# Splits, ropes, partial sums and an activation table issued in another order in a retention/GLA decoder layer

## The chip, the core and the metric

The kernel runs on one core of one Trainium2 chip. The metric is device time in microseconds (us) of one execution; several executions are timed and the median is given. A core has engines that run side by side, each with its own queue in program order: TensorE (PE, with its weight loads PEld), VectorE (DVE), ScalarE (ACT), GpSimd (POOL), and SyncE (SP), which here only issues DMAs. POOL issues DMAs too, those that add into their destination among them.

## The reference

One layer over 528 positions (16 meta tokens and 512 of the sequence), width 1024, float32:

```python
u = rms_norm(h, norm_gain)
proj = u @ w_in
(rq, rk, rv, rg, gq, gk, gv, gg, glr, m_ret, m_gla) = jnp.split(proj, points, axis=-1)
rq = rope(rq, pos); rk = rope(rk, pos) * RET_QK_DIM ** -0.5
o_ret = head_group_norm(retention_chunked(rq, rk, rv), ret_norm_gain) * silu(rg)      # 4 heads
log_a = log_sigmoid(glr @ w_gate_up + b_gate) / GLA_GATE_TAU
o_gla = head_rms_norm(gla_chunked(gq * GLA_K_DIM ** -0.5, gk, gv, log_a), gla_norm_gain) * silu(gg)
merged = sigmoid(m_ret) * (o_ret @ w_branch_ret) + sigmoid(m_gla) * (o_gla @ w_branch_gla)
h = h + merged @ w_out
return rms_norm(h, final_norm_gain)[:, N_META:]
```

## The kernel before

Every product of float32 operands is made from three matmuls: `split(hi, lo, src)` (L154) rounds a tile on ACT (`scalar.copy`, the CAST rows of L155) and takes the rest on DVE (`tensor_sub`, the TENSOR_TENSOR rows of L155); PE then multiplies hi by hi, hi by lo and lo by hi. Weights come from DRAM by SP in tiles of 512 KB (`wraw`, six buffers) and are split into `whi` and `wlo` (`wsplit`, three buffers each).

Most projections go through `quad` (L253): it computes a block of two column tiles over two token halves with seven products, each on sums of weight blocks, as in Strassen's scheme, where eight would be plain. `product(i, ...)` splits its weight block and issues 24 matmuls of 256 columns. The products come in the order 1, 2, 6, 7, 5, 4, 3, with a `yield` behind each. The sums of weight blocks (`w11 += x3`, L320; `w21 += w11`, L325) are DVE additions, and partial results are copied from a bank of PSUM by ACT (`copy`, L300) before the bank is used further: the bank of products 1, 6, 5 and 3 is `b`, that of 7 and 4 is `c`. `proj_a` (L350) is the plain projection used for the first pair of GLA heads, q (gq0) and then k (gk0): 96 matmuls each.

The text of the kernel is made of generators. `weave(dense, chain)` (L205) advances `chain` by one step after each step of `dense`, so that chains of small operations (gates, rope, scores, attention) lie between dense matmuls. `tick` (L233), called once at each dense step, counts down the entries of the list `pend` and calls those at zero, from the head of the list on, stopping at the first that is not due. A planner orders each engine's queue: it takes the operations by their place in this text and by when its own model of costs has their inputs ready. `after(ins, prev)` pins one instruction behind another on the same engine; `act` and `vec` chain instructions so with the last of their engine in `ends`, and `qsplit` is a split whose two halves are chained so.

The places that matter here, in order of time:

- The forget gates of GLA (`forget_gates`, L641): z = glr @ w_gate_up in five matmuls, then for each of the five blocks Abs, Exp and Identity on ACT and two operations on DVE, then a scaling of gv (L674) and five Ln on ACT with a DVE subtraction each (L678). This chain is woven into `gla_qk(0)`; gk0's two weight halves are split inside `proj_a`, behind the chain's z blocks. The next dense stage is the first output gate of GLA, `gla_g(0)` (names gg).
- For each retention head h: `ret_qk(h)` (names rqk) woven with the attention of the head before; `ret_rope(h)` (rpk, rpq, on DVE), `ret_g(h)` (output gate, names rg), `ret_v(h)` (names rv) and `ret_scores(h)`. The attention of a head has six steps: four blocks of values (av) and two of `turn` (L426), which transposes on PE (ot) and splits on ACT and DVE (oh L439, ol L440). For h = 0 and h = 3 the gate and values are the dense part, and rope runs through `every(gen, 3, 2)`, which puts a pause behind each two steps.
- `gates_ret` (L1124, names mr): the last gates. `part` (L1131) reads partial sums kr from DRAM, multiplies by the gate on DVE (L1132) and adds the product back by a POOL DMA. The sums of the first two pairs are due 4 and 5 ticks after the start, the others 2 ticks after their gate. `gate` (L894) evacuates a product, scales it and applies Sigmoid (L898).

Of the kernel before, what the change touches and what calls it, by code (L numbers as in the profile page):

```python
# [11 lines left out]

# [8 lines left out]
F32 = mybir.dt.float32  # L21
# [6 lines left out]
P = 128  # L28
# [79 lines left out]
def hybrid_kernel(ctx: ExitStack, tc: tile.TileContext, I, out: bass.AP):  # L108
# [105 lines left out]
    def every(gen, n, m=1):  # L214

        for i, _ in enumerate(gen):
            yield
            if i % m == m - 1:
                for _ in range(n - m):
                    yield  # L220
# [32 lines left out]
    def quad(cols, rows, name, evac, meta=None, adds=True):  # L253
# [26 lines left out]
        def product(i, form, w, ps, fresh):  # L280
            hi, lo = wsplit([P, 4, 256], f"{name}_{i}")
            split(hi, lo, w)
            for t in range(2):
                col = slice(t * P, (t + 1) * P)
                for kk in range(4):
                    u = [f[form][:, kk, col] if rows else f[form][:, kk, :256] for f in (fh, fl)]
                    v = [f[:, kk, :] if rows else f[:, kk, col] for f in (hi, lo)]
                    first = fresh and kk == t == 0
                    for j, (x1, x2) in enumerate(((0, 0), (0, 1), (1, 0))):
                        l, r = (u[x1], v[x2]) if rows else (v[x1], u[x2])  # L290
                        m = nc.tensor.matmul(ps[:, t, :], l, r, start=first and j == 0, stop=kk == 3 and j == 2,  # L291
                                             skip_group_check=not fresh or t == 1)
                        if t == kk == j == 0:
                            pin(m)
            order[:] = [m]
# [17 lines left out]
        run_late()  # L313
        yield
# [4 lines left out]
        product(2, A12, w21, a, True)  # L319
# [30 lines left out]
    def proj_a(col, meta, name, evac):  # L350
# [8 lines left out]
        for kh in range(2):  # L359
            if (name, kh) not in loaded:  # L360
                load_a(col, kh, name)
            if (name, kh) not in parts:
                parts[name, kh] = wsplit([P, 4, 256], f"{name}_{kh}")
                (qsplit if name == "gk0" else split)(*parts[name, kh], loaded.pop((name, kh)))
# [276 lines left out]
    def forget_gates():  # L641
# [11 lines left out]
        yield  # L653
        for b in range(5):
# [6 lines left out]
            nc.scalar.activation(e, ps, AF.Abs)  # L661
            nc.scalar.activation(e, e, AF.Exp, scale=-1.0)

            nc.scalar.activation(w1, e, AF.Identity, bias=one)
            nc.vector.scalar_tensor_tensor(w1, w1, 1.0, e, op0=ALU.subtract, op1=ALU.subtract)
# [3 lines left out]

        for _ in range(4):  # L670
            yield
        last = ends["act"]
# [285 lines left out]
    def rope(t, c, name):  # L958
# [5 lines left out]
        nc.vector.tensor_mul(m[0], t[:, 0], c[0])  # L964
        nc.vector.tensor_mul(m[1], t[:, 1], c[1])
# [22 lines left out]
    def ret_rope(h):  # L988
        q, k = R["raw", h]
        yield from rope(k, (cs[:, 0], cs[:, 1]), f"rpk{h}")  # L990
# [16 lines left out]
    def ret_g(h):  # L1007
        sg = rp.tile([P, NTB, 512], F32, tag="sg", name=f"sg{h}")
        R["sg", h] = sg
        yield from quad((C_RG + h * 512, C_RG + h * 512 + 256), True, f"rg{h}", rows_into(sg, AF.Silu))  # L1010
# [113 lines left out]
    def gates_ret():  # L1124
# [6 lines left out]
        def part(k, c, s):  # L1131
            nc.vector.tensor_mul(k, k, sigr[c][:, :, s])  # L1132
            collect(kept[:, 2 * c:2 * c + 2, s], k, False)

        for c in range(2):
            k = rp.tile([P, 2, T], F32, tag=("sh", "sl")[c], name=f"kr{c}")
            nc.gpsimd.dma_start(k, kept2[:, 2 * c:2 * c + 2, :])
            pend.append((4 + c, lambda c=c, k=k: part(k, c, slice(0, T))))

# [25 lines left out]
    for h in range(4):  # L1165
        if h == 0:
            drain(ret_qk(h))
        else:
            weave(ret_qk(h), ret_attention(h - 1))
# [4 lines left out]
        else:  # L1174
            weave(run(ret_g(h), ret_v(h)), run(every(ret_rope(h), 3, 2), ret_scores(h)))
# [97 lines left out]
```

## Time and profile before

| what | value |
|---|---|
| median of 3 runs | 792.84 us (792.55 to 793.69) |
| profiled execution | 790.81 us, its span 789.0 us |
| PE busy in the span | 770.7 us (98%) |
| PEld | 700.0 us (89%) |
| DVE | 571.7 us (72%) |
| ACT | 450.1 us (57%) |
| POOL | 143.5 us (18%) |
| granted PE clock, mean | 0.994 |

A busy PE is counted while a matmul is in its pipeline, so 98% says how little of the span PE stood with nothing to do, not that it ran at its peak. A row of a timeline reads: start, duration, engine, line, operation, output<-inputs, shape, how many in a row; in brackets the idle time of the engine before it and what ended it.

### The profile page before, as it was taken

The page shows a single profiled execution, that of the slowest core. Times are in us where ns is not written, and L with a number is a line of the kernel's source. Part 1 is how long each engine was busy: PE and PEld are TensorE (multiplying, and loading weights), DVE is VectorE, ACT ScalarE, POOL GpSimd, SP SyncE. Part 2 cuts the span into 40 slices and gives each one's busy share as a digit, 9 for nine tenths or more (in the row PEclk, how much of TensorE's full clock was granted, in tenths as well). Part 3 has the DMA queues.
Part 4 walks back from the last instruction along what each step waited for, and adds up shares of the span by engine and source line. Part 5 has one row for each costly group of instructions (what it writes and reads, how often), then busy time and mean ns, then how long its engine had stood idle before and what let it go on. Part 6 is the DMA issues. An engine that isn't in the chain of part 4 may idle for free.

```text
span 789.0 us, 13628 instructions
## 1 busy us (share of the span) xinstructions
PE 770.7 (98%) x5404; PEld 700.0 (89%) x5404; DVE 571.7 (72%) x824; ACT 450.1 (57%) x744; POOL 143.5 (18%) x200
## 2 busy tenths in 40 slices
PE   9989999999999999999999999999999899989996
PEld 6779989999888899999989999889999898888885
DVE  5858688677654579788977688977686988577832
ACT  8887775577555456645646545646445655363422
POOL 2310120101312313100320100340011101333031
PEclk9989999999999999999999999999999999999999
DMA  9882503653138983833585463695465326799202
GB/s 283 263 206 46 141 5 105 142 142 91 67 124 198 252 189 108 184 110 107 168 246 145 111 160 108 160 237 138 123 150 129 101 88 205 118 310 313 94 2 107
DMA packets 94600, 117.91 MB, mean 149 GB/s; under 512 B 5956, under 2 KB 80580, under 8 KB 94280
## 3 DMA queue, kind: packets, MB, share of 16 engines
q1 hardware_dynamic: 74456, 85.32, 35.4%
q0 software_dynamic: 19936, 31.46, 20.7%
q8 instruction: 42, 0.69, 0.4%
q10 hardware_dynamic: 144, 0.26, 0.1%
q14 instruction: 22, 0.18, 0.1%
HBM read 99.20 MB, written 17.83 MB: 148 GB/s over the span
## 4 chain that ended last, share of the span: by engine, by line
PE 85%; DVE 6%; ACT 3%; DMA 2%; issue 2%; POOL 1%; POOLq 0%; SPq 0%; DVEq 0%; ACTq 0%
PE rv_b L291 6%; PE rg_b L291 5%; PE rqk_b L291 4%; PE br_p L193 4%; PE br_p L194 4%; PE br_p L190 4%; PE mg_b L291 3%; PE gv_p L557 3%; PE rg_c L291 3%; PE rv_c L291 2%; PE gg_b L291 2%; PE rqk_c L291 2%; PE mr_b L291 2%; PE bg_p L190 2%; PE bg_p L194 2%; PE bg_p L193 2%
## 5 line engine op out<-in xcount | busy, mean ns | idle before, releaser
L194 PE MATMUL br_p<-oh,br_l 128*128 128x512 f32 x128 | 50.5, 395 | 0.0
L193 PE MATMUL br_p<-ol,br_h 128*128 128x512 f32 x128 | 50.5, 395 | 0.0
L190 PE MATMUL br_p<-oh,br_h 128*128 128x512 f32 x128 | 50.5, 395 | 0.0
L155 ACT CAST rv_h<-rv_w 128x1024 fp32r<-128x1024 f32 x24 | 25.2, 1052 | 28.0 <-DVE rv_w L320 10.1
L891 POOL DMA_DIRECT2D kept<-mt x24 | 20.4, 849 | 110.5 <-ACT mt L1153 110.5
L1093 ACT ACTIVATE on<-av,nm,g_r 128x512 f32<-128x512 f32 x16 | 12.5, 779 | 48.6 <-DVE nm L1091 48.6
L155 DVE TENSOR_TENSOR rv_l<-rv_w,rv_h 128x1024 fp32r<-128x1024 f32 x24 | 29.3, 1222 | 8.8 <-ACT rv_h L155 8.8
L155 DVE TENSOR_TENSOR rg_l<-rg_w,rg_h 128x1024 fp32r<-128x1024 f32 x20 | 24.4, 1220 | 7.9 <-ACT rg_h L155 7.9
L194 PEld LDWEIGHTS br_p<-oh,br_l 128*128 128x128 f32 x128 | 24.0, 187 | 5.8
L193 PEld LDWEIGHTS br_p<-ol,br_h 128*128 128x128 f32 x128 | 24.0, 188 | 5.2
L190 PEld LDWEIGHTS br_p<-oh,br_h 128*128 128x128 f32 x128 | 24.0, 188 | 5.1
L271 POOL DMA_DIRECT2D rqk_x<-in_w_in_dram x8 | 10.4, 1306 | 98.6 <-DVE vl L155 83.1
L155 DVE TENSOR_TENSOR rqk_l<-rqk_w,rqk_h 128x1024 fp32r<-128x1024 f32 x20 | 24.4, 1219 | 5.1 <-ACT rqk_h L155 5.1
L291 PE MATMUL rg_b<-rg_l,fh 128*128 128x256 f32 x96 | 27.0, 282 | 0.3 <-DVE rg_l L155 0.3
L155 ACT CAST rg_h<-rg_w 128x1024 fp32r<-128x1024 f32 x20 | 21.0, 1052 | 11.0 <-PE br_p L193 5.0
L291 PE MATMUL rqk_b<-fh,rqk_l 128*128 128x256 f32 x96 | 27.1, 283 | 0.1
L291 PE MATMUL rqk_b<-fh,rqk_h 128*128 128x256 f32 x96 | 27.2, 283 | 0.0
L291 PE MATMUL rqk_b<-fl,rqk_h 128*128 128x256 f32 x96 | 27.0, 282 | 0.0
L291 PE MATMUL rv_b<-rv_h,fl 128*128 128x256 f32 x96 | 27.0, 282 | 0.0
L291 PE MATMUL rv_b<-rv_l,fh 128*128 128x256 f32 x96 | 27.0, 281 | 0.0
L291 PE MATMUL rg_b<-rg_h,fh 128*128 128x256 f32 x96 | 27.0, 281 | 0.0
L291 PE MATMUL rv_b<-rv_h,fh 128*128 128x256 f32 x96 | 27.0, 281 | 0.0
(646 smaller groups left out, 3171.6 us busy)
## 6 DMA issues: line engine op xcount, KB each, us to landing
rv_w<-in_w_in_dram SPq DMA_DIRECT2D x16, 512.0 KB, 4.1
br_w<-in_w_branch_ret_dram SPq DMA_DIRECT2D x16, 512.0 KB, 3.7
rqk_w<-in_w_in_dram SPq DMA_DIRECT2D x12, 512.0 KB, 5.0
rg_w<-in_w_in_dram SPq DMA_DIRECT2D x12, 512.0 KB, 4.0
kept<-mt POOLq DMA_DIRECT2D x24, 256.0 KB, 5.1
bg_w<-in_w_branch_gla_dram SPq DMA_DIRECT2D x8, 512.0 KB, 3.9
mr_w<-in_w_in_dram SPq DMA_DIRECT2D x8, 512.0 KB, 3.7
kept<-gb POOLq DMA_DIRECT2D x16, 256.0 KB, 4.1
```

What stands on the lines that cost most here:

```text
L155: return nc.scalar.copy(hi, src), nc.vector.tensor_sub(lo, src, hi.bitcast(F32))
L190: m = nc.tensor.matmul(o, lh, rh, start=first, stop=False)
L193: nc.tensor.matmul(o, lh, rl, start=False, stop=False)
L194: m = nc.tensor.matmul(o, ll, rh, start=False, stop=last)
L271: nc.gpsimd.dma_start(t, block(0, 1), accum_op=ALU.add)
L291: m = nc.tensor.matmul(ps[:, t, :], l, r, start=first and j == 0, stop=kk == 3 and j == 2, skip_group_check=not fresh or t == 1)
L557: m = nc.tensor.matmul(pss[t], (al if j == 1 else ah)[t // 2, kh][:, k, c], (lo if j == 2 else hi)[:, kk, :], start=q == kk == j == 0, sto ...
L891: nc.gpsimd.dma_start(dst, t, **({} if first else {"accum_op": ALU.add}))
L1093: nc.scalar.activation(on, ps, AF.Identity, scale=r, bias=nm)
```

## The change

Four edits. The split of both k weight halves (gk0) moves from `proj_a` into `forget_gates`, ahead of the z matmuls, one half to a step; the Abs and the first DVE operation of each gate block are pinned behind the last of these splits; four empty steps of the chain go, and Ln and the scaling of gv are pinned behind the last Exp. `quad` can split the weights of its second product ahead of the yield (`ahead`); this is used in `ret_g(0)` and `ret_g(3)`, and there the first two rope products are pinned behind that split (`low[1]`). The attention of head 2 gives only five of its six steps to `ret_qk(3)`; the sixth, the second `turn`, is run in the first pause of `every` in the stage of `ret_g(3)`. In `gates_ret` the multiplication of `part` is pinned behind the DVE half of the last split issued so far, and a Sigmoid of one column is put into `pend` with count 3, behind the two entries with 4 and 5, pinned behind the ACT half of the last split issued.

```diff
--- before.py
+++ after.py
@@ -9,6 +9,7 @@
 
 
 from contextlib import ExitStack
+from itertools import islice
 
 import numpy as np
 
@@ -211,12 +212,14 @@
         for _ in chain:
             pass
 
-    def every(gen, n, m=1):
+    def every(gen, n, m=1, other=None):
 
         for i, _ in enumerate(gen):
             yield
             if i % m == m - 1:
                 for _ in range(n - m):
+                    if other is not None:
+                        next(other, None)
                     yield
 
     def run(*gens):
@@ -250,7 +253,9 @@
         return (wp.tile(shape, F32R, tag="whi", name=f"{name}_h", bufs=3),
                 wp.tile(shape, F32R, tag="wlo", name=f"{name}_l", bufs=3))
 
-    def quad(cols, rows, name, evac, meta=None, adds=True):
+    low = []
+
+    def quad(cols, rows, name, evac, meta=None, adds=True, ahead=False):
 
 
 
@@ -277,9 +282,13 @@
 
         b, a, c = [ppt(f"{name}_{x}").rearrange("p (t c) -> p t c", t=2) for x in "bac"]
 
-        def product(i, form, w, ps, fresh):
+        def prepare(i, w):
             hi, lo = wsplit([P, 4, 256], f"{name}_{i}")
-            split(hi, lo, w)
+            low[:] = split(hi, lo, w)
+            return hi, lo
+
+        def product(i, form, w, ps, fresh, ready=None):
+            hi, lo = ready or prepare(i, w)
             for t in range(2):
                 col = slice(t * P, (t + 1) * P)
                 for kk in range(4):
@@ -311,12 +320,13 @@
         product(1, A11, w11, b, True)
         x = copy(b, 1)
         run_late()
+        ready = prepare(2, w21) if ahead else None
         yield
         if not adds:
             x3 = wraw(f"{name}_x3")
             nc.vector.tensor_add(x3, w22, w12)
             nc.vector.tensor_add(x1, w12, w11)
-        product(2, A12, w21, a, True)
+        product(2, A12, w21, a, True, ready)
         nc.vector.tensor_add(w11, w11, x3)
         evac(0, 0, a, x)
         yield
@@ -357,11 +367,11 @@
             pss = [[p[:, th * 256:(th + 1) * 256] for th in range(2)] for p in full]
         n = HT if meta else 256
         for kh in range(2):
-            if (name, kh) not in loaded:
-                load_a(col, kh, name)
             if (name, kh) not in parts:
+                if (name, kh) not in loaded:
+                    load_a(col, kh, name)
                 parts[name, kh] = wsplit([P, 4, 256], f"{name}_{kh}")
-                (qsplit if name == "gk0" else split)(*parts[name, kh], loaded.pop((name, kh)))
+                split(*parts[name, kh], loaded.pop((name, kh)))
             hi, lo = parts.pop((name, kh))
             for th in range(2):
                 for t in range(2):
@@ -651,6 +661,12 @@
         act(nc.scalar.copy(wzs, wz))
         vec(nc.vector.tensor_sub(wzs[64:96], wz[64:96], wzs[64:96].bitcast(F32)))
         yield
+
+        for kh in range(2):
+            load_a(C_GK, kh, "gk0")
+            parts["gk0", kh] = wsplit([P, 4, 256], f"gk0_{kh}")
+            qsplit(*parts["gk0", kh], loaded.pop(("gk0", kh)))
+            yield
         for b in range(5):
             ps = pat(f"z{b}")
             nc.tensor.matmul(ps, gl[:, b * P:(b + 1) * P], wzs, start=True, stop=True)
@@ -658,18 +674,15 @@
                         bufs=4 if b < 4 else 2).rearrange("p a b -> p (a b)")
             es.append(e)
             w1 = w1s[:, b % 2]
-            nc.scalar.activation(e, ps, AF.Abs)
-            nc.scalar.activation(e, e, AF.Exp, scale=-1.0)
+            after(nc.scalar.activation(e, ps, AF.Abs), ends["act"])
+            last = nc.scalar.activation(e, e, AF.Exp, scale=-1.0)
 
             nc.scalar.activation(w1, e, AF.Identity, bias=one)
-            nc.vector.scalar_tensor_tensor(w1, w1, 1.0, e, op0=ALU.subtract, op1=ALU.subtract)
+            x = nc.vector.scalar_tensor_tensor(w1, w1, 1.0, e, op0=ALU.subtract, op1=ALU.subtract)
+            after(x, ends["vec"])
             nc.vector.scalar_tensor_tensor(la[:, b, :], ps, 0.0, w1, op0=ALU.min, op1=ALU.add)
             if b % 2:
                 yield
-
-        for _ in range(4):
-            yield
-        last = ends["act"]
         for t in range(NTB):
             after(nc.scalar.activation(gv0[:, t, :], gv0[:, t, :], AF.Copy, scale=rt[:, t:t + 1]), last)
         for b in (4, 0, 1, 2, 3):
@@ -955,14 +968,18 @@
     def tmp2(name):
         return tmp(name).rearrange("p (a b) -> p a b", a=2)
 
-    def rope(t, c, name):
+    def rope(t, c, name, prev=None):
 
         def view(m):
             return m[:, :t.shape[2] * t.shape[3]].rearrange("p (h c) -> p h c", h=2)
 
         m = [view(rp.tile([P, 2 * HT], F32, tag="tmp", name=f"{name}_{i}", bufs=7)) for i in range(4)]
-        nc.vector.tensor_mul(m[0], t[:, 0], c[0])
-        nc.vector.tensor_mul(m[1], t[:, 1], c[1])
+        x = nc.vector.tensor_mul(m[0], t[:, 0], c[0])
+        if prev is not None:
+            after(x, prev)
+            after(nc.vector.tensor_mul(m[1], t[:, 1], c[1]), prev)
+        else:
+            nc.vector.tensor_mul(m[1], t[:, 1], c[1])
         nc.vector.tensor_sub(m[0], m[0], m[1])
         yield
         nc.vector.tensor_mul(m[2], t[:, 1], c[0])
@@ -987,7 +1004,7 @@
 
     def ret_rope(h):
         q, k = R["raw", h]
-        yield from rope(k, (cs[:, 0], cs[:, 1]), f"rpk{h}")
+        yield from rope(k, (cs[:, 0], cs[:, 1]), f"rpk{h}", None if h % 3 else low[1])
         kh = rp.tile([P, 2, 2, HT], F32R, tag="kh", name=f"kh{h}")
         kl = rp.tile([P, 2, 2, HT], F32R, tag="kl", name=f"kl{h}")
         for i, m in enumerate(R[f"rpk{h}"]):
@@ -1007,7 +1024,8 @@
     def ret_g(h):
         sg = rp.tile([P, NTB, 512], F32, tag="sg", name=f"sg{h}")
         R["sg", h] = sg
-        yield from quad((C_RG + h * 512, C_RG + h * 512 + 256), True, f"rg{h}", rows_into(sg, AF.Silu))
+        yield from quad((C_RG + h * 512, C_RG + h * 512 + 256), True, f"rg{h}", rows_into(sg, AF.Silu),
+                        ahead=h % 3 == 0)
 
     def ret_v(h):
         vh = rp.tile([P, NTB, 512], F32R, tag="vh", name=f"vh{h}")
@@ -1129,13 +1147,15 @@
                 nc.sync.dma_start(sigr[c], sig[:, 2 * c:2 * c + 2, :])
 
         def part(k, c, s):
-            nc.vector.tensor_mul(k, k, sigr[c][:, :, s])
+            after(nc.vector.tensor_mul(k, k, sigr[c][:, :, s]), low[1])
             collect(kept[:, 2 * c:2 * c + 2, s], k, False)
 
         for c in range(2):
             k = rp.tile([P, 2, T], F32, tag=("sh", "sl")[c], name=f"kr{c}")
             nc.gpsimd.dma_start(k, kept2[:, 2 * c:2 * c + 2, :])
             pend.append((4 + c, lambda c=c, k=k: part(k, c, slice(0, T))))
+        one = sp.tile([P, 1], F32, tag="one", name="sig1")
+        pend.append((3, lambda: after(nc.scalar.activation(one, mhalf, AF.Sigmoid), low[0])))
 
         def evac(n, th, p, q):
             s = slice(th * 256, (th + 1) * 256)
@@ -1166,13 +1186,14 @@
         if h == 0:
             drain(ret_qk(h))
         else:
-            weave(ret_qk(h), ret_attention(h - 1))
+            at = ret_attention(h - 1)
+            weave(ret_qk(h), at if h < 3 else islice(at, NTB + 1))
         if h % 3:
             weave(turns(gates_gla(h - 1), ret_branch(h - 1)), ret_rope(h), skip=2)
             weave(ret_g(h), ret_scores(h))
             drain(ret_v(h))
         else:
-            weave(run(ret_g(h), ret_v(h)), run(every(ret_rope(h), 3, 2), ret_scores(h)))
+            weave(run(ret_g(h), ret_v(h)), run(every(ret_rope(h), 3, 2, at if h else None), ret_scores(h)))
     weave(run(ret_branch(2), gates_ret()), every(ret_attention(3), 2))
     mh, ml = [[cp.tile([P, 4, T], F32R, tag=f"x{n}0", name=f"m{n}0"),
                *[cp.tile([P, 2, T], F32R, tag=f"f{n}{i}", name=f"m{n}{i}") for i in (S2, S3)]] for n in "hl"]
```

## The prediction

> **What bounds the kernel now.** I read the page first, then the waits of TensorE (PE), then the ten-microsecond windows, then the timeline of each engine in the three stretches that the waits point at.
>
> ```profile
> span 789.0 us, 13628 instructions
> ```
>
> The waits of PE, longest first: engine, line, tile, then what it waited for, microseconds in total, times, longest.
>
> ```profile
> PE gk_p L373 <- ACT gk_h L155: 2.2, 1, 2.2
> PE rg_a L291 <- DVE rg_l L155: 1.4, 1, 1.4
> PE warm_p L528 <- DVE warm L525: 1.2, 1, 1.2
> PE mr_b L291 <- ACT mr_x L300: 1.1, 1, 1.1
> PE gm L806 <- DVE lal L155: 1.0, 1, 1.0
> PE mr_c L291 <- ACT mr_x L300: 0.7, 1, 0.7
> PE gk_p L373 <- DVE gk_l L155: 0.6, 1, 0.6
> PE gv_p L557 <- ACT gv_h L155: 0.6, 1, 0.6
> PE mr_b L291 <- DVE mr_l L155: 0.5, 1, 0.5
> PE z L656 <- DVE la L666: 0.5, 1, 0.5
> PE rg_c L291 <- DVE rg_l L155: 0.4, 1, 0.4
> PE rg_b L291 <- DVE rg_l L155: 0.3, 1, 0.3
> ```
>
> PE is the bound: over 789.0 us these waits make 10.5 us. Of them the change aims at gk_p (2.2 and 0.6, with z 0.5 ahead of it), the rg group (1.4, 0.4, 0.3) and the mr group (1.1, 0.7, 0.5): 7.7 us. More lies in the speed of PE behind the first:
>
> ```profile
> 50.00:60.00 10.00, 7.84 (x40) 7.54 (x41) 7.98 (x12) 9.97 (x16) 0.00 (x0) 0.66 0.74 157
> ```
>
> This is the window from 50 to 60 us (busy time of PE, weight load, DVE, ACT, POOL; then the granted clock): 0.66, where nearly every other window has 1.00. So the pause before the k projection is paid twice, as waiting and as slow matmuls.
>
> **Part 1, k weights ahead of the gate chain.** First how much there is to gain.
>
> ```profile
> 48.03 0.28 PE L373 MATMUL gq_p<-xh,gq_l 128*128 128x256 f32 x1
> 48.83 0.50 PE L656 MATMUL z<-fg_wz,fg_b 128*128 128x512 f32 x1 [0.52 <-DVE la L666]
> 51.55 0.39 PE L373 MATMUL gk_p<-xh,gk_h 128*128 128x264 f32 x1 [2.22 <-ACT gk_h L155]
> ```
>
> The chain of waits gives the end of that projection:
>
> ```profile
> 53.08 13.97 PE gk_p L373 x92
> 67.05 2.84 PE gg_b L291 x24
> ```
>
> The q projection's last matmul starts at 48.03. If the k weights lie ready, k can start at about 48.4 (one pitch, and 0.25 us for one z matmul). Its 96 matmuls (2 halves of the contraction, 2 token halves, 2 column tiles, 4 blocks, 3 products) need 0.12 each at full clock, an estimate from the gg_b row (2.84 us for 24), so 11.5 us: they would end at 59.9 where gg_b now starts at 67.05. Ceiling: 7.1 us, of it 3.1 from waiting before 51.55 and 4.0 from inside (0.6 waiting, the rest clock).
>
> Now whether ACT and DVE allow it. ACT's queue (brackets: idle time just before, and what ended it):
>
> ```profile
> 41.46 0.68 ACT L535 ACTIVATE gvm<-gvm_s,rt 16x512 f32<-16x512 f32 x1 [1.80 <-PE gvm_s L449]
> 44.12 1.08 ACT L661 ACTIVATE fg_e<-z 128x512 f32<-128x512 f32 x2 [1.97 <-PE z L656]
> ...
> 50.44 1.06 ACT L155 CAST gk_h<-gk_w 128x1024 fp32r<-128x1024 f32 x1
> ...
> 61.04 1.04 ACT L155 CAST gg_h<-gg_w 128x1024 fp32r<-128x1024 f32 x1
> ```
>
> The moved step issues two loads, two casts of 1.06 and two DVE subtractions. The casts are queued behind gvm, whose end is near 42.1, and ACT stands idle from there to 44.12: two casts, 2.1 us, fill that gap and delay the gate chain by about 0.1. The loads:
>
> ```profile
> 32.37 1.70 SPq L347 DMA_DIRECT2D gk_w<-in_w_in_dram  x2
> ```
>
> ```profile
> gk_w<-in_w_in_dram SPq DMA_DIRECT2D x2, 512.0 KB, 7.4
> ```
>
> Issued from 32.37 and landing 7.4 later (median), they are there about 41, so a cast at 42.1 does not wait, and the Abs activations now pinned behind it do not either. On SP they keep their place, ahead of the gg loads; raw buffers come free earlier, which only lets later loads start sooner. POOL is not passed.
>
> The gate chain itself: now it fills ACT from 44.12 to 61.04, 16.9 us, with 2.1 of k casts inside; 14.8 without. In the new emission the first two z matmuls stand behind 72 instead of 66 q matmuls, so the chain starts about 0.7 later (44.8) and its Ln ends at 59.6. The next PE work, the first output gate (gg_b), needs a gg_h cast and a gg_l subtraction. Two ways. Where the planner of queues puts the gg_h cast in a gap of the chain, as it now puts gk_h at 50.44 among the gate activations, PE goes on at 59.9: gain 7.1, of which I give back 0.6 since DVE then has the la subtractions, gg_l and the gate evacuations in less time: 6.5. Where the cast stays behind Ln, as in the row at 61.04, gg_h ends at 60.7, gg_l about 1.2 later, and PE waits from 59.9 to 62.0: 5.0. I take 6.5, because the gap that took gk_h in is still there and gg_h is the next cast in line. A loss I exclude: both ways leave PE ahead of 67.05. With the clock low again (a rival below) 1.6 remains, the low end.
>
> **Part 2, rope and the late turn, last head (and rope alone, first head).** DVE's queue in the stretch:
>
> ```profile
> 611.92 0.87 DVE L440 SCALAR_TENSOR_TENSOR ol<-ot,rgain,oh 128x256 fp32r<-128x256 f32 x2
> 612.71 0.69 DVE L965 TENSOR_TENSOR rpk<-k,cs 128x528 f32<-128x528 f32 x1
> 613.32 1.22 DVE L155 TENSOR_TENSOR rg_l<-rg_w,rg_h 128x1024 fp32r<-128x1024 f32 x1
> ...
> 639.77 1.23 DVE L155 TENSOR_TENSOR rv_l<-rv_w,rv_h 128x1024 fp32r<-128x1024 f32 x1
> ```
>
> The second product's rg_l is late by 1.4 because two pairs of L440 (0.87 a pair) and two rope products (0.69 each; the rows show one of either kind) stand before it, about 3 us. Split ahead, rope behind it, and the second turn after the third product: rg_l comes 3 us sooner, the 1.4 goes, and with it the 0.3 and 0.4 behind. But the timeline shows DVE without a gap from here to the rv_l at 639.77, and PE takes that one the moment it ends. Nothing is taken off DVE: the 1.7 us of L440 is only moved behind a later product, with its PE transposes and ACT casts. So what is late next is rg_l of the fifth product or rv_l at 639.77, and PE gains only as far as it has score or meta-row matmuls to run in that wait. Ceiling 2.1 (1.4 + 0.4 + 0.3), floor minus 1.7 (the two pairs before a split that PE waits for). I take 1.3, nearer the ceiling since independent matmuls exist there. For the first head there is no wait to remove and rope only changes places: 0.
>
> **Part 3, partial sums behind splits, Sigmoid early.** DVE, then ACT:
>
> ```profile
> 695.42 1.23 DVE L1132 TENSOR_TENSOR kr<-kr,sigr 128x1024 f32<-128x1024 f32 x1 [4.09 <-DMA kr<-kept]
> 696.56 1.22 DVE L155 TENSOR_TENSOR mr_l<-mr_w,mr_h 128x1024 fp32r<-128x1024 f32 x1
> 698.45 1.23 DVE L1132 TENSOR_TENSOR kr<-kr,sigr 128x1024 f32<-128x1024 f32 x1 [0.67 <-DMA kr<-kept]
> ```
>
> ```profile
> 701.24 0.87 ACT L439 ACTIVATE oh<-ot,rgain 128x256 fp32r<-128x256 f32 x2 [5.64 <-DVE ol L440]
> 702.00 1.04 ACT L155 CAST mr_h<-mr_w 128x1024 fp32r<-128x1024 f32 x1
> 703.06 1.28 ACT L898 ACT_TABLE_LOAD   x1
> 704.35 0.63 ACT L898 ACTIVATE sigr<-sigr 128x512 f32<-128x512 f32 x1
> 704.89 0.57 ACT L300 COPY mr_x<-mr_b 128x512 f32<-128x512 f32 x1
> ```
>
> DVE stands 4.09 us for a load from DRAM (kr) with mr_l queued behind: PE loses 0.5. Behind both kr products stands L440, for that ACT stands 5.64, and the copies that free PE's banks come late: 1.1 and 0.7. The first sum is now pinned behind the split of the fourth product in order (product 7), the second behind product 5: mr_l and L440 pass the DMA wait, ACT gets to its copies in time. All of 2.3 can go; I take 2.3. What then follows on POOL is the accumulating store of each sum, later by up to the 2 us that the second sum is, and the loads queued behind it. Floor: minus 4.1, one more DVE stand of the length of the first.
>
> The early Sigmoid does not come early. It is appended with count 3 behind entries with 4 and 5, and the list is emptied from its head only, so it is emitted at the fifth step, after two true Sigmoids, and is pinned behind product 5's cast. The 1.28 load falls once either way: 0. Without a row for a one-column activation I bound it by the 0.63 row, in ACT time that is not on the path.
>
> **Sum.** 6.5 + 1.3 + 2.3 = 10.1 us. The profiled execution took 790.81 us (span 789.0 and 1.8 around it), 2.0 below the median of the runs, 792.84; I take the saving from the median: 782.7.
>
> **Rivals.**
> ACT takes the place: the gg_h cast stays behind Ln; 5.0 + 1.3 + 2.3 = 8.6, so 784.2. For it: the order at 61.04. Against it: gk_h at 50.44.
> The same with the clock low again: PE then idles about 2.1 us, as long as the 2.2 that preceded the low clock in the trace, and loses again what the clock cost there, 4.0 less the 0.6 waited, 3.4: 787.6. The row at 51.55 with the window's 0.66 speaks for it; that other waits (1.4 at rg_a) left the clock at full speaks against.
> By the Trainium skill (TensorE: Matmul & The Clock Gate, "What's actually happening") the clock falls to half only after an idle window of about 3.4 us; a 2.1 us wait would then keep the clock and this rival would end at 784.2. The trace disagrees so far that the fall came after 2.2 us of unbroken idling.
> DVE and DMA give parts 2 and 3 back: 6.5 alone, 786.3. For it: the gapless DVE.
> Slower: the sums stand DVE in part 3. If the four half-size sums each waited for their kr load as the first did (4.09), DVE would stand 16.4 us; two products of 2.85 cover 5.7, PE loses 10.7, and the kernel ends at 792.84 - 7.8 + 10.7 = 795.7. It decides from 9.4 us of lost PE time on (7.8 and the 1.6 of a measurable loss). Against it: each sum is now issued later after its load, not sooner.
>
> **How the numbers follow.** About 0.2% (1.6 us) is what a measurement can tell. Chances: forecast 0.50 (its own range 780.5 to 784); ACT in the way, full clock 0.16; with low clock 0.12; parts 2 and 3 given back 0.11; all gains eaten by queue orders that shift in untouched stages, within 1.6 us of before, 0.06; slower 0.05. Range 780.5 (ceilings: 7.1 + 2.1 + 2.3 = 11.5 makes 781.3, less run scatter) to 788, which leaves out some 0.15. Faster 0.89, same 0.06, slower 0.05.
>
> **What would show it.** Part 1: two gk_h casts between 42 and 44.2, no wait of gk_p, granted clock 1.00 from 50 to 60, gg_b from about 60. A wait of gg_b for gg_h or gg_l is the first rival. Part 2: no wait of rg_a; if a wait of rg_b or rv_b for DVE of like size comes up, it was moved. Part 3: mr_l before kr on DVE, no wait of mr_b or mr_c for mr_x; the table load still at a true Sigmoid. I am wrong if PE's waits in 60 to 80 or 620 to 645 grow by what goes elsewhere, or if stages between, which the change doesn't touch, come out in another order.

## Result and profile after

The changed kernel takes 785.42 us (median of 4 runs, 784.39 to 786.95) beside 793.09 for the kernel before in the same session: ratio 0.9905, interval 0.9883 to 0.9926. It is faster by 7.7 us; forecast were 10.1. The profiled execution took 786.95 us, its span 785.2.

The waits of PE in the kernel after (engine, line, tile, what was waited for; total us, times, longest). Line numbers have moved by 1 to 20: L155 is L156 now, L291 is L300, L1132 is L1150, L1159 is L1179.

```profile
PE wo_p L191 <- DVE mt L1178: 2.8, 4, 1.3
PE rqk_b L300 <- ACT oh L449: 1.3, 1, 1.3
PE warm_p L538 <- DVE warm L535: 1.2, 1, 1.2
PE rg_b L300 <- DVE rg_l L156: 1.0, 1, 1.0
PE rqk_b L300 <- ACT rqk_x L309: 0.9, 1, 0.9
PE rqk_b L300 <- DVE rqk_l L156: 0.6, 1, 0.6
PE br_p L191 <- ACT mh L156: 0.5, 1, 0.5
```

All waits that the change aimed at are gone: gk_p, rg_a, rg_c, mr_b, mr_c. In their place stand two of rqk_b (for oh and rqk_l) and one of rg_b in the last head, one of rqk_b in the first (for rqk_x), and at the very end br_p and wo_p.

**The first stage came out as forecast.** The window from 50 to 60 us, then ACT's timeline:

```profile
50.00:60.00 10.00, 10.00 (x83) 9.95 (x83) 8.82 (x14) 9.45 (x14) 0.00 (x0) 1.00 0.22 62
```

```profile
41.77 1.98 ACT L156 CAST gk_h<-gk_w 128x1024 fp32r<-128x1024 f32 x2
44.55 1.09 ACT L677 ACTIVATE fg_e<-z 128x512 f32<-128x512 f32 x2 [0.81 <-PE z L672]
...
51.76 0.58 ACT L677 ACTIVATE fg_e<-z 128x512 f32<-128x512 f32 x1
52.24 1.04 ACT L156 CAST gg_h<-gg_w 128x1024 fp32r<-128x1024 f32 x1
...
58.19 3.18 ACT L689 ACTIVATE fg_e<-fg_e,one 128x512 f32<-128x512 f32 x5
```

PE has no gap and a granted clock of 1.00 (0.66 before). Both k casts lie in ACT's old gap, and the gg_h cast went in at 52.24, ahead of Ln. PE's timeline shows what that gives, the start of the first gate product:

```profile
59.77 0.28 PE L300 MATMUL gg_b<-gg_h,xh 128*128 128x256 f32 x1
```

**The mr stage lost its waits as forecast, and the end paid for it.** From the first matmul of mr_b to the first of br_p PE took 24.75 us before (690.33 to 715.08) and takes 21.62 now (685.49 to 707.11). From there to the start of the last wo_p matmul it took 66.41 (to 781.49) and takes 71.08 (to 778.19). PE's rows with a wait, in the stretch from 724 us on:

```profile
724.58 0.48 PE L191 MATMUL br_p<-oh,br_h 128*128 128x512 f32 x1 [0.49 <-ACT mh L156]
730.97 0.47 PE L191 MATMUL wo_p<-wo_h,mh 128*128 128x512 f32 x1 [0.56 <-DVE mt L1178]
733.21 0.50 PE L191 MATMUL wo_p<-wo_h,mh 128*128 128x512 f32 x1 [0.64 <-DVE mt L1178]
736.15 0.50 PE L191 MATMUL wo_p<-wo_h,mh 128*128 128x512 f32 x1 [1.28 <-DVE mt L1178]
738.12 0.50 PE L191 MATMUL wo_p<-wo_h,mh 128*128 128x512 f32 x1 [0.30 <-DVE mt L1178]
```

The brackets add up to 3.27 us, the stage grew by 4.67. A bracket counts from the modelled end of the matmul before (0.39 after its start), while the pitch of back-to-back matmuls here is 0.23: a bracket hides some 0.16, and the matmul after a wait starts the next one about 0.1 late. Five waits make 1.3, and 3.3 and 1.3 explain 4.6 of the 4.7.

Why DVE is late stands in its own timeline, and in POOL's:

```profile
713.19 0.69 DVE L1179 TENSOR_TENSOR mt<-mt,mk 128x512 f32<-128x512 f32 x1 [1.84 <-DMA mk<-kept]
...
718.48 0.69 DVE L1178 TENSOR_TENSOR mt<-sigr,br_p 128x512 f32<-128x512 f32 x1 [3.23 <-PE br_p L195]
...
723.14 0.69 DVE L1179 TENSOR_TENSOR mt<-mt,mk 128x512 f32<-128x512 f32 x1 [2.83 <-DMA mk<-kept]
```

```profile
696.46 2.16 POOL L1164 DMA_DIRECT2D kr<-kept  x3 [8.07 <-DMA kept<-mt]
698.61 0.98 POOL L904 DMA_DIRECT2D kept<-kr  x1
706.89 0.57 POOL L1177 DMA_DIRECT2D mk<-kept  x1 [7.30 <-DMA kept<-kr]
707.53 5.83 POOL L904 DMA_DIRECT2D kept<-kr  x5
711.88 2.07 POOL L1177 DMA_DIRECT2D mk<-kept  x1
720.30 0.58 POOL L1177 DMA_DIRECT2D mk<-kept  x1 [6.34 <-DMA kept<-kr]
```

In the kernel before, DVE stood only once for more than 1 us here, also for a reload, and PE had no wait of br_p or wo_p:

```profile
727.25 0.69 DVE L1159 TENSOR_TENSOR mt<-mt,mk 128x512 f32<-128x512 f32 x1 [4.09 <-DMA mk<-kept]
```

DVE needs mk, the reload of a sum. POOL issues it only when that sum has been added back (kept<-kr). Between the first reload and the second now stand the other five accumulates in one block; before, the six went out between 696.95 and 720, one at a time but for the last two. The stand of 3.23 at 718.48 is put down to PE here, but in a second profile of this kernel the same instruction stands 3.98 and the last to come is an accumulate (kept<-kr) that still reads the buffer it wants. The issues with their sizes and median time to landing, before and after:

```profile
kept<-kr POOLq DMA_DIRECT2D x4, 256.0 KB, 7.6
```

```profile
kept<-kr POOLq DMA_DIRECT2D x4, 256.0 KB, 10.7
```

The windows of the kernel after tell the rest: DVE is busy 4.25 of 10 us from 710 to 720, where it stands for reloads and buffers, and 9.88 from 730 to 740, where it works off the backlog and PE falls to 7.22.

```profile
710.00:720.00 10.00, 10.00 (x45) 8.01 (x44) 4.25 (x7) 2.37 (x3) 3.96 (x4) 1.00 1.12 221
...
730.00:740.00 10.00, 7.22 (x28) 4.72 (x27) 9.88 (x15) 3.96 (x6) 0.54 (x1) 1.00 0.46 148
```

### The profile page after: what moved, and what is told of

Its sections match the earlier page's. It is cut to its first block, busy times and chain, and to the rows that moved or that the text cites. A ratio compares the mean times of both kernels' runs of the same rounds, so it can differ in the third digit from the quotient of the medians.

```text
span 785.2 us, 13632 instructions
## 1 busy us (share of the span) xinstructions
PE 768.7 (98%) x5404; PEld 696.5 (89%) x5404; DVE 571.2 (73%) x824; ACT 450.2 (57%) x745; POOL 144.7 (18%) x200
## 4 chain that ended last, share of the span: by engine, by line
PE 73%; DMA 8%; DVE 6%; issue 6%; ACT 4%; POOL 2%; POOLq 0%; SPq 0%; ACTq 0%; DVEq 0%
PE rg_b L300 5%; PE rv_b L300 5%; PE rqk_b L300 4%; PE gv_p L567 3%; PE rg_c L300 3%; PE mg_b L300 3%; PE br_p L191 3%; PE br_p L195 3%; PE br_p L194 3%; PE rqk_c L300 2%; PE rv_c L300 2%; PE gg_b L300 2%; PE wo_p L191 2%; DMA kept<-gb 2%; PE wo_p L195 2%
## 5 line engine op out<-in xcount | busy, mean ns | idle before, releaser
L156 ACT CAST rv_h<-rv_w 128x1024 fp32r<-128x1024 f32 x24 | 25.3, 1053 | 29.1 <-DVE rv_w L330 10.2
L156 DVE TENSOR_TENSOR rv_l<-rv_w,rv_h 128x1024 fp32r<-128x1024 f32 x24 | 29.4, 1223 | 8.8 <-ACT rv_h L156 8.8
L156 DVE TENSOR_TENSOR rg_l<-rg_w,rg_h 128x1024 fp32r<-128x1024 f32 x20 | 24.4, 1222 | 7.9 <-ACT rg_h L156 7.9
L191 PE MATMUL wo_p<-wo_h,mh 128*128 128x512 f32 (+1 forms) x72 | 26.9, 374 | 2.8 <-DVE mt L1178 2.8
L156 DVE TENSOR_TENSOR rqk_l<-rqk_w,rqk_h 128x1024 fp32r<-128x1024 f32 x20 | 24.4, 1221 | 7.0 <-ACT rqk_h L156 7.0
L300 PE MATMUL rqk_b<-fh,rqk_h 128*128 128x256 f32 x96 | 27.2, 283 | 2.1 <-ACT oh L449 1.3
L156 ACT CAST rg_h<-rg_w 128x1024 fp32r<-128x1024 f32 x20 | 21.0, 1052 | 14.3 <-PE br_p L194 5.0
L276 POOL DMA_DIRECT2D rqk_x<-in_w_in_dram x8 | 10.5, 1310 | 98.5 <-PE rv_b L300 65.7
L300 PE MATMUL rg_b<-rg_l,fh 128*128 128x256 f32 x96 | 27.1, 282 | 1.0 <-DVE rg_l L156 1.0
L300 PE MATMUL rqk_b<-fh,rqk_l 128*128 128x256 f32 x96 | 27.0, 282 | 0.6 <-DVE rqk_l L156 0.6
L300 PE MATMUL rg_b<-rg_h,fh 128*128 128x256 f32 x96 | 27.0, 282 | 0.0
L156 ACT CAST br_h<-br_w 128x1024 fp32r<-128x1024 f32 x16 | 16.8, 1050 | 17.8 <-issue 7.4
L300 PE MATMUL rg_b<-rg_h,fl 128*128 128x256 f32 x96 | 27.0, 281 | 0.0
L300 PE MATMUL rv_b<-rv_h,fl 128*128 128x256 f32 x96 | 27.0, 281 | 0.0
```

Of the source, the lines that this page charges most:

```text
L156: return nc.scalar.copy(hi, src), nc.vector.tensor_sub(lo, src, hi.bitcast(F32))
L191: m = nc.tensor.matmul(o, lh, rh, start=first, stop=False)
L276: nc.gpsimd.dma_start(t, block(0, 1), accum_op=ALU.add)
```

## The parts by themselves

Four kernels, with the kernel before timed beside them (median 792.13, 790.29 to 795.17). Theory: part 1 carries the gain, and parts 2 and 3 move their waits. Rival: all three give what was forecast, and something between them is lost.

**Part 1 alone**

```diff
+        for kh in range(2):
+            load_a(C_GK, kh, "gk0")
+            parts["gk0", kh] = wsplit([P, 4, 256], f"gk0_{kh}")
+            qsplit(*parts["gk0", kh], loaded.pop(("gk0", kh)))
+            yield
...
+            after(nc.scalar.activation(e, ps, AF.Abs), ends["act"])
```

> Part 1 alone (k weights split ahead of the gate chain), on the kernel before. Theory (part 1 carries the whole gain, parts 2 and 3 give theirs back): 6.5 us off, ratio 0.992, about 786.5, so within 1.5 us of the whole change. Rival (all three parts give what the sum said, and something else ate 3.6): 6.5 off too, but then the other two parts alone must show 1.3 and 2.3. Rival (part 1 gives more than it was priced, 9 or 10 us, and the others lose): 783.5. In the profile: no wait of gk_p, clock 1.00 from 50 to 60, gg_b from about 60.

785.57 us (784.92 to 786.09), ratio 0.991, interval 0.9892 to 0.9928: 6.6 us. gg_b starts at 60.41, against 66.89 in the kernel before.

**Part 2 alone**

```diff
+                        ahead=h % 3 == 0)
...
+            weave(ret_qk(h), at if h < 3 else islice(at, NTB + 1))
...
+            weave(run(ret_g(h), ret_v(h)), run(every(ret_rope(h), 3, 2, at if h else None), ret_scores(h)))
```

> Part 2 alone (weights of the second gate product split ahead, rope pinned behind, second turn of head 2 moved into the gate stage), on the kernel before. Theory (DVE has no gap in that stretch, so a wait is only moved): within 1 us of 793, rg_a waits for nothing, and rg_b or rv_b waits for DVE instead, 1 to 2 us in sum. Rival (the wait goes for good, as the sum had it): 1.3 to 2.1 us off, 791.0 to 791.7, and the waits of the rg and rv groups in sum under 1 us.

792.8 us (791.3 to 795.38), ratio 1.0005, interval 0.9992 to 1.0018: nothing, and at most 0.6 us of gain. PE's rows with a wait in the last head (590 to 640 us), of the kernel before and of this one:

```profile
614.59 0.39 PE L291 MATMUL rg_a<-rg_l,xh 128*128 128x256 f32 x1 [1.38 <-DVE rg_l L155]
618.74 0.38 PE L291 MATMUL rg_b<-rg_l,fh 128*128 128x256 f32 x1 [0.30 <-DVE rg_l L155]
622.24 0.38 PE L291 MATMUL rg_c<-rg_l,fh 128*128 128x256 f32 x1 [0.41 <-DVE rg_l L155]
```

```profile
607.46 0.36 PE L300 MATMUL rqk_b<-fh,rqk_h 128*128 128x256 f32 x1 [0.42 <-ACT oh L449]
608.50 0.38 PE L300 MATMUL rqk_b<-fh,rqk_l 128*128 128x256 f32 x1 [0.57 <-DVE rqk_l L156]
618.29 0.39 PE L300 MATMUL rg_b<-rg_l,fh 128*128 128x256 f32 x1 [0.98 <-DVE rg_l L156]
```

That is 2.09 us of waits before and 1.97 with part 2. The wait of rg_a has become one of rg_b, and without the second turn in the rqk stage two of rqk_b have opened. The 0.57 for rqk_l is explained by the order on PE: the eight transposes of the second turn (1.04 us from 605.94 on) had been what PE did while DVE made that rqk_l. The 0.42 for oh varies from profile to profile; it is taken up again below. DVE shows no gap from about 606 to 625 us in either trace. On an engine as full as this one, another order only picked which product waits.

**Part 3 alone**

```diff
+            after(nc.vector.tensor_mul(k, k, sigr[c][:, :, s]), low[1])
...
+        pend.append((3, lambda: after(nc.scalar.activation(one, mhalf, AF.Sigmoid), low[0])))
```

> Part 3 alone (partial sums pinned behind splits, Sigmoid table early), on the kernel before. Theory (the chain of accumulating DMAs of the partial sums takes over): the mr waits, 2.3 us, go, but PE waits for mt or mh in the last branch and the output projection by 1.5 to 4 us: 791 to 794. Rival (the gain stands): 790.5, no wait of br_p or wo_p over 0.3 us.

792.35 us (791.41 to 795.34), ratio 1.0003, interval 0.9989 to 1.0017: nothing. mr takes 21.62 us instead of 24.75, the end 71.17 instead of 66.41.

**Parts 1 and 2**

```diff
-            after(nc.vector.tensor_mul(k, k, sigr[c][:, :, s]), low[1])
+            nc.vector.tensor_mul(k, k, sigr[c][:, :, s])
...
-        pend.append((3, lambda: after(nc.scalar.activation(one, mhalf, AF.Sigmoid), low[0])))
```

> The change without part 3. Theory (part 3 gives nothing): 785 to 786.5, no faster or slower than the whole change by over 1 us, mr waits of 2 to 3 us back, and no waits of wo_p. Rival (part 3 is worth its 2.3): 787.5 or more, slower than the whole change by 2 us. If the whole change's slow runs (near 786.7, beside 784.4) come from the DMA chain of part 3, these runs should agree within 1 us.

784.47 us (783.49 to 785.17), ratio 0.9898, interval 0.9878 to 0.9918: no worse than the whole change. Its times spread over 1.7 us, those of the whole change over 2.6, so part 3 is not the only source of scatter. The rival falls: part 1 is the gain, and the others add nothing to it that these intervals can tell.

## Was it the pause that lowered the clock?

```diff
+        if name == "gk0":
+            for _ in range(18):
+                m = nc.tensor.matmul(pss[0][1], ah[0, 0][:, 0, :P], ah[0, 0][:, 0, :HT], start=True, stop=True)
+                after(m, fill[0])
```

> The kernel before with 18 filler matmuls of 264 columns (about 2.0 us at full clock) between the last z matmul and the first of the k projection, in the 2.2 us in which PE waits for the k weights' first half; their results are overwritten. PE is then idle for at most some 0.3 us there. Theory (the pause lowers the clock): the granted clock from 50 to 60 us, 0.66 before, is 0.95 to 1.00, the k projection's body shrinks by 2.7 to 3.4 us, and the time is about 789.2. The Trainium skill (TensorE: Matmul & The Clock Gate, What's actually happening) puts a fall of the clock to an idle window of about 3.4 us; by it 2.2 us of pause are not its cause. Rival (the low clock comes from something other than the pause, for example the load of the stage): 0.66 stays, and the time is 792.1, or up to 2 us worse if the fillers run into the k projection.

```profile
49.07 2.33 PE L362 MATMUL gk_p<-xh 128*128 128x264 f32 x18
```

```profile
50.00:60.00 10.00, 9.41 (x75) 8.98 (x74) 7.97 (x12) 9.97 (x15) 0.00 (x0) 1.00 0.69 155
```

The clock is 1.00 (the column after the five engines), and gg_b starts at 64.02 instead of 66.89: 2.9 us for the clock alone, since the real work starts only 0.1 sooner. So the pause lowers it. The Trainium skill's rule (TensorE: Matmul & The Clock Gate, "What's actually happening") puts the fall to an idle window of about 3.4 us. As an unbroken idle of that length the trace does not bear it out: PE idled 0.52 us, ran one z matmul and idled 2.22.

The price of this pause is not the same each time. Followed in windows of 0.1 us, the clock is at 0.50 from 52.0 to 58.8 us in the kernel before (6.8 us) and from 51.3 to 58.2 in the profile of part 2 alone (6.8 us), where it falls before the pause is over. In the profile of part 3 alone, whose first stage has the same text and the same pause (2.23), it is at 0.50 only from 54.2 to 57.6 (3.4 us): the window from 50 to 60 has 0.83, and the k projection takes 14.2 us from its first matmul to gg_b, against 15.3 before and 12.6 with the fillers.

The time missed its expectation: 791.35 us (789.15 to 792.69), ratio 0.9985, interval 0.9973 to 0.9996, a gain of 1.1 us. Of the 2.87 at gg_b, 1.87 are left when the first retention head starts and 1.21 after a wait of rqk_b for ACT there (0.49) that the profile of the kernel before does not have. How often the kernel before pays the smaller price was not counted.

## What sets the end

Six more kernels start from the changed one. PE's time in mr and at the end, from starts of matmuls as above:

| kernel | mr | end | sum |
|---|---|---|---|
| before | 24.75 | 66.41 | 91.16 |
| after | 21.62 | 71.08 | 92.70 |
| after, run again | 21.59 | 70.44 | 92.03 |
| part 1 alone | 24.40 | 67.49 | 91.89 |
| part 2 alone | 24.50 | 67.65 | 92.15 |
| part 3 alone | 21.62 | 71.17 | 92.79 |
| parts 1 and 2 | 24.36 | 67.26 | 91.62 |
| sums not pinned | 25.62 | 66.47 | 92.09 |
| kr loads on SP | 21.60 | 70.20 | 91.80 |
| residual loads late | 21.60 | 70.25 | 91.85 |
| reloads one ahead | 21.63 | 70.97 | 92.60 |
| those three together | 21.62 | 68.21 | 89.83 |
| no accumulates | 21.60 | 66.43 | 88.03 |

The end takes 66.4 to 67.7 us in the five kernels without the pin (before, part 1 alone, part 2 alone, parts 1 and 2, sums not pinned) and 70.4 to 71.2 in the three profiles with the pin and nothing else changed there.

**Sums not pinned, Sigmoid kept early**

```diff
-            after(nc.vector.tensor_mul(k, k, sigr[c][:, :, s]), low[1])
+            nc.vector.tensor_mul(k, k, sigr[c][:, :, s])
```

> The changed kernel with the partial sums not pinned behind the splits (the early Sigmoid stays). Theory (the pin, through the order on DVE and POOL, causes the waits at the end): the mr waits of before return (0.86 to 1.1, 0.33 to 0.7, 0.5 to 0.74; 2 to 3 us in sum), the waits of br_p and wo_p at the end shrink from 3.3 us to about 0.6, and the time is that of parts 1 and 2 without part 3, about 784.5. Rival (the early Sigmoid, on ACT, makes them): the mr waits are gone or not, the waits at the end stay near 3 us, and the time is 785.4 or, with the mr waits back as well, about 788.

784.46 us (783.31 to 786.39), ratio 0.9895, interval 0.9878 to 0.9912. The waits of mr are back (1.5 + 1.3 + 0.4), those of the end are gone: it is the pin, not the Sigmoid by itself. The 256 KB accumulates land in 7.5 us again.

**No accumulates of the sums**

```diff
-            collect(kept[:, 2 * c:2 * c + 2, s], k, False)
```

> The changed kernel without the accumulation of the partial sums of the first three heads' retention outputs into the kept buffer (their accumulate DMAs from POOL are left out, so those sums are missing from the output; loads, products and pins stay). Theory (accumulates behind the kr loads on POOL make the sums late): the reloads of the sums no longer wait for an accumulate, the waits of br_p and wo_p at the end go from 3.3 us to below 0.7, and the gain in mr stays: 782 to 783. Rival (DVE's order alone makes them late): waits of 2 to 3 us stay, 785.

779.64 us (779.06 to 780.69), ratio 0.9835, interval 0.9819 to 0.9852. Its longest waits of PE (two of 0.2 follow), and the window in which the others fall behind:

```profile
PE warm_p L538 <- DVE warm L535: 1.2, 1, 1.2
PE rg_b L300 <- DVE rg_l L156: 1.0, 1, 1.0
PE rqk_b L300 <- DVE rqk_l L156: 0.6, 1, 0.6
```

```profile
710.00:720.00 10.00, 10.00 (x45) 8.01 (x44) 9.18 (x14) 4.39 (x6) 2.16 (x4) 1.00 0.52 154
```

DVE works 9.18 of these 10 us instead of 4.25, mr keeps its gain and the end takes 66.43, as before. So the accumulates are needed for the late end, and the order on DVE alone does not make it. The edit takes away their place on POOL, their traffic and the buffers they hold all at once, and the order of before was not run without accumulates, so what the pin would be worth in their absence is not shown.

**kr loads on SP: is it POOL's order?**

```diff
-            nc.gpsimd.dma_start(k, kept2[:, 4 + 2 * n:6 + 2 * n, s])
+            nc.sync.dma_start(k, kept2[:, 4 + 2 * n:6 + 2 * n, s])
```

> The changed kernel with one edit: the four loads of kr halves in the last rope move from POOL's queue to SP's. In the changed kernel's trace the accumulate of the first partial sum stands behind these loads on POOL (loads from 696.46, accumulates at 698.61 and 707.53, reload of the sum at 706.89 and 720.30), and PE waits at the end for the last products of the sums: br_p 0.49, wo_p 0.56+0.64+1.28+0.30, together 3.3 us. Theory (POOL's order is what part 3 pays with): the accumulates are issued about 2 us earlier, the reloads too, and most of the 3.3 us go: 782.5 (782 to 783.5) with the mr waits still gone. Rival 1 (the sums are late because PE now arrives earlier, not because of the queue): the same 3.3 us of waits, 785.4. Rival 2 (SP's own queue holds the kr loads back behind its collections): a new wait of DVE for kr, rv or mr late by 1 to 3 us, 786 to 788.

784.28 us (783.77 to 784.99), ratio 0.9893, interval 0.9874 to 0.9912. The accumulates do go out sooner, the first at 690.48 instead of 698.61 (7.5 us after the start of mr instead of 13.1), and still the second reload lands late:

```profile
720.41 0.69 DVE L1179 TENSOR_TENSOR mt<-mt,mk 128x512 f32<-128x512 f32 x1 [7.65 <-DMA mk<-kept]
```

The theory that these loads alone hold the sums back falls. The accumulates no longer go out in one block here (698.95, 702.78 and 707.92), and those of 256 KB still take 10.8 us to land.

**Residual loads late: is it traffic?**

```diff
-            nc.sync.dma_start(hs[half], I["x"][:, half * 512:(half + 1) * 512].rearrange("(t p) d -> p t d", p=P))
+            after(nc.sync.dma_start(hs[half], I["x"][:, half * 512:(half + 1) * 512].rearrange("(t p) d -> p t d", p=P)), merge[-1])
```

> The changed kernel with one edit: the two 1 MB loads of the residual (hs), which go out on SP at 682 just ahead of the last branch's weights, are put behind the eight output weights (wo_w). In the changed kernel the accumulates of the sums land after a median of 10.7 us and the reloads after up to 11.2 us, where before they took 7.6 and up to 7.3. Theory (DMA traffic at the end: with mr faster, the accumulates meet loads that came later before): without 2 MB in that stretch accumulates land in 7 to 8 us, the reloads in at most 8, the waits of br_p and wo_p go from 3.3 us to below 1.5, and the time is about 783 (782 to 784). Rival (the order on POOL and DVE sets them): the landing times shorten or not, the waits stay near 3 us, 785. A loss is possible if hs lands late for the first residual sum (about 750): then DVE waits for hs and the time is above 786.

783.37 us (782.29 to 785.1), ratio 0.9894, interval 0.9879 to 0.9909. The time lies in the range of the theory, but not by its mechanism: the 256 KB accumulates still take 10.9 us to land and the end is 70.25, so this traffic by itself is not it either.

**Reloads one product ahead**

```diff
+            if c < KD and c not in mk:
+                mk[c] = tmp(f"mk{c}")
+                nc.gpsimd.dma_start(mk[c], kept[:, c, :])
...
+                reload(c)
+                reload(c + 1)
+                k = mk[c]
```

> The changed kernel with one edit: the reloads of the sums (mk) are issued one product ahead, so that the second stands on POOL before the last four accumulates and not behind them. In the changed kernel DVE stands 1.84, 2.83 and 0.60 us for the first three reloads (in the variant with the kr loads on SP 7.65 us for the second). Theory (order on POOL: a reload waits behind accumulates that it does not need): the stand for the second reload goes, and the waits of br_p and wo_p shrink from 3.3 us to below 1.5: about 783. Rival (DMA traffic or the backlog of DVE sets them, whatever the order): the stand moves to the third reload, which needs the second sum, and 2 to 3 us of PE waits stay: 785.

783.75 us (782.04 to 786.06), ratio 0.9891, interval 0.9873 to 0.9909. The end is 70.97. DVE now stands once for a reload and once for a buffer that an accumulate still reads (products, reloads and kr halves share a ring of seven):

```profile
714.32 0.69 DVE L1187 TENSOR_TENSOR mt<-mt,mk 128x512 f32<-128x512 f32 x1 [3.76 <-DMA mk<-kept]
...
721.20 0.69 DVE L1186 TENSOR_TENSOR mt<-sigr,br_p 128x512 f32<-128x512 f32 x1 [4.81 <-DMA kept<-kr]
```

The rival said that the stand would move, and it did, but to a buffer and not to the third reload.

**All three edits together**

> The changed kernel with the three edits together: kr loads on SP, residual loads behind the output weights, reloads one product ahead. Both theories of the end expect the waits of br_p and wo_p below 1 us with the mr waits still gone, and so 781.5 to 782.5, the fastest so far; the kernel without accumulates, 779.6, is a floor for it. If the kr loads behind the last branch's weights on SP now come late, mr keeps its gain but the sums do not, and the time is 784.

782.28 us (781.42 to 783.21), ratio 0.9877, interval 0.9862 to 0.9891. The wait of br_p is gone and 1.2 us of wo_p are left; DVE still stands 3.42 us for a buffer that an accumulate reads, and for no reload. This is the fastest complete kernel here by its median; its interval does not touch that of the changed kernel timed beside it (it does touch the first one, 0.9883 to 0.9926):

> The changed kernel as it is, beside the three others on one chip. Its four times were 784.4, 784.5, 786.4 and 787.0, and the profiled one was the last of these. If the spread is luck of transfers (the stand of 1.29 us of rqk_b for oh in the last head, which the kernels with one edit at the very end do not show), this profile has less of it and a span of about 783; the waits of br_p and wo_p, by either theory, stay between 2.5 and 3.5 us; median 785.

785.99 us (782.77 to 786.64), ratio 0.9918, interval 0.9902 to 0.9934. Its profiled execution was the fastest of the six, 782.77, as the first one of this kernel had been the slowest of four, 786.95. The 4.2 us between the two come up in three places, 1.3 in the first head's rqk stage, 2.2 in the last one's and 0.7 at the end. In the first head ACT stands for an accumulate (kept<-gb), 6.33 us in the first profile and 3.89 in the second, with the copy rqk_x behind it. POOL in the last head, in the first profile and in the second:

```profile
592.24 1.34 POOL L276 DMA_DIRECT2D rg_x<-in_w_in_dram  x1 [7.02 <-DMA rg_x<-in_w_in_dram]
```

```profile
588.74 1.34 POOL L276 DMA_DIRECT2D rg_x<-in_w_in_dram  x1 [4.91 <-DMA rg_x<-in_w_in_dram]
```

POOL stands for a transfer of 5 to 7 us, and behind it in its queue is the power that the attention's normalisation needs; where it stands longer, ACT's oh and so rqk_b (1.29) are late. In the ten profiles with part 2 the wait follows this stand: none up to 5.07 us, 0.26 to 0.42 from 5.23 to 5.51, and 1.29 at 7.02. In the four without part 2 the stand is 5.09 to 5.66 and rqk_b never waits for oh. So the size of that wait is chance, but it is part 2 that lets it through. The 0.57 and the 0.98 are in every profile with part 2 (of the others, only the one with the fillers has a like wait for rqk_l, 0.51, at the longest stand of the four).

## Why the prediction was right and wrong

The sum said 10.1 us and the change gives 7.7. The time lies in the stated range because that reached up to the rivals (788); it lies outside the forecast's own part of it (780.5 to 784). Of the three terms one held.

- **Part 1, 6.5: right, in size and by its steps.** 6.6 by itself. gg_b was to start at 59.9 and starts at 59.77. The branch taken for the gg_h cast, into a gap of the gate chain, is the one that came. Ln ends later than I had it (61.4, not 59.6), which costs nothing since only the first rival had PE waiting for it.
- **The clock.** That the pause before gk_p is paid twice is shown by the fillers; the second payment is 2.9 us in that pair of profiles where I had 3.4, and about 1.7 in the profile of part 3 alone; in the median time the fillers gave 1.1. With no new pause, the rival with the low clock did not come up.
- **Part 2, 1.3: wrong, it is 0.** The working itself said that DVE has no gap and that nothing is taken off it, and named rg_l of the fifth product and rv_l as next. The step that failed is the choice behind it: nearer the ceiling "since independent matmuls exist there". Matmuls that had covered a wait there were the transposes of the second turn, and the change moves just those: the cover of one wait (0.57) went with the removal of another, and rg_b now waits 0.98 for a DVE that has no less to do.
- **Part 3, 2.3: wrong, it is 0, though its mechanism in the mr stage was right** and larger than said: 3.1, since each of the three waits costs PE about 0.26 more than its bracket shows (the 0.16 and 0.1 worked out above). The failed step is that the later accumulates cost nothing. The sentence named them, "later by up to the 2 us", with the loads queued behind, and followed them no further. From there it is one more step to the end: accumulate, reload, DVE, wo_p. It took 4.0 to 4.7 us in the two profiles of the changed kernel against the kernel before, and at least 2.8 against every kernel without the pin. The floor I gave, one DVE stand of 4.1, is near that size by luck: it was meant for a load in the mr stage, not for the end.
- **The early Sigmoid** does come early, against what I said: emitted at the fifth step, it was put right behind the cast it is pinned to, and so ahead of the first true one, by the planner of ACT's queue, since that cast starts as early as 692.18.

```profile
693.25 1.28 ACT L1158 ACT_TABLE_LOAD   x1
694.55 0.20 ACT L1158 ACTIVATE sig<-mhalf 128x1 f32<-128x1 f32 x1
...
695.98 0.63 ACT L911 ACTIVATE sigr<-sigr 128x512 f32<-128x512 f32 x1
```

  Its worth by itself was not tried; where it stands without the pin, mr is no shorter (25.62).
- **The rivals.** The one in which parts 2 and 3 are given back, 786.3, is what happened (part 1 alone takes 785.57), by DVE in part 2 and by DMA and DVE in part 3. It had 0.11; a full DVE and two floors below nothing were reasons for more. The slower kernel, with each sum standing DVE in the mr stage, did not come up: DVE has no stand for kr there any more.

**What stays open.** The accumulates, later and closer together with the pin, make the end late: leaving them out or leaving the pin out mends it. Which part of that is POOL's order, which the reload's place, which their longer landing and which the ring of seven buffers is not told apart: each of three edits alone leaves the end at 70.2 to 71.0 us, together they bring it to 68.21. A larger ring was not tried, though DVE stands for a buffer that an accumulate reads in the second profile of the changed kernel (3.98), with the reloads ahead (4.81) and with all three edits (3.42). Why the 256 KB accumulates land in a median of 10.5 to 11.3 us in every profile with the pin and in 7.5 to 8.0 in every one without it was not tried by itself.

## What to carry to other kernels

A pause of PE can cost twice, as waiting and as a low clock behind it, so a split that can go ahead of a long ACT chain is worth more than its wait. On an engine without a gap, as DVE in part 2, pinning chose who waits: look for what takes work off it, or for matmuls that cover the wait, and count those that the change itself moves away. And when an edit makes a store later, follow it to its reader (store, reload, the engine that stands for it, PE), however many microseconds further on that lies.

## Unexpected on the hardware

A 2.2 us pause of PE (with 0.5 just before it) was enough to halve the granted clock, for 6.8 us in two profiles and for 3.4 in a third; filled, the clock stays 1.00. Accumulating transfers of 256 KB took a median of 7.5 to 8.0 us to land in the six profiles without the pin and 10.5 to 11.3 in the seven with it, also where they did not go out in one block. And one kernel's executions spread from 782.8 to 787.0 us through the luck of transfers in two stages, so that the size of a wait in a single profile (1.29 us for oh) can be no measure of what the change costs.
